# High and low activations as one 512-column operand in the transposed dense products of a two-block kernel

## The chip, the cores and the metric

The kernel runs on one core of a Trainium2 chip. The metric is the device time of one execution in microseconds; less is better. The engines are called as in the profile: PE (TensorE, with PEld for its weight loads), DVE (VectorE), ACT (ScalarE), POOL (GpSimd) and SP (SyncE, which starts the DMAs).

## The reference

The input is x, 256 tokens of 1024 values, and a memory of 256 tokens. Two blocks follow each other, all in fp32. The first has two layers, and the second two hybrid layers (gated sums of three attentions) with projections of their own.

```python
for l in range(DEPTH):
    h = h + 0.5 * swiglu_ffn(rms_norm(h, ffn1_norm[l]), ffn1_w_in[l], ffn1_w_out[l])
    h = h + hybrid_mixer(rms_norm(h, mix_norm[l]), ...)
    h = h + memory_cross_attention(rms_norm(h, xattn_norm[l]), rms_norm(mem, mem_norm[l]), ...)
    h = h + 0.5 * swiglu_ffn(rms_norm(h, ffn2_norm[l]), ffn2_w_in[l], ffn2_w_out[l])
```

`swiglu_ffn` is `(silu(gate) * up) @ w_out` with `gate, up = split(x @ w_in)`, 1024 to 2 x 2816 and back. Most of the arithmetic is such products of 256 tokens with a weight matrix of 1024 or more rows.

## The kernel before

**Precision.** A product x @ w is made of three, with each operand split in a high part, rounded to the matmul's fp32r, and a low part, the rest: high by high, high by low and low by high. Activations are split where they are made (an ACT copy for the high part, a DVE subtraction for the low one). Weights are split as they arrive, by `Weights` (lines 484 to 558): the DMA brings 4 row pieces of 128 at a time into `raw` (three buffers), and `splits` makes of every two pieces a pair `wh` (ACT) and `wl` (DVE), 128x1024 each, in four buffer pairs. A pair comes free when the matmuls that `take` hands it to have been issued.

**Dense steps.** `lin` (605) makes tokens x outputs, with activations as the stationary operand. `lin_T` (631) makes the transposed result, outputs x tokens: weights are the stationary operand, 128x128 a piece, and the 256 tokens of an activation tile (`Xt`, 130) are streamed. For a step of 512 outputs it takes two PSUM banks (`banks_T`, 628), each with two chunks of 128 outputs side by side, and for every row piece c of the weights `chunk_T` (621) makes 4 chunks x 3 matmuls of 256 columns. When all pieces are done, all four chunks are. `lin_halves` (645) is the same over two steps whose row pieces are taken by halves; the output products of mixer, cross attention and hybrid layers use it.

The banks of tag "a" are four (`psa`, 363), so the next step has two of its own while the last one's are emptied. `ps_a` (392) takes one, `give` (389) marks one as free.

**What reads the results.** For each step a `done` function starts a routine that empties the banks two chunks at a time: in `ffn` (819) `gate` multiplies with the broadcast inverse root of the norm (`rsb`, made by `Norm.finish` and `spread`, waited for in `scale_b`) and takes silu; `up` multiplies with that and splits the product for the second matrix; `to_h` (797) scales the output product and adds it to the residual hT, and starts the next norm, whose high and low parts are the next stage's activations. `conv_done`, `sb_done`, `gl_done` and `up_done` do the like in the mixer and in the hybrid layers.

**Order.** A planner (`Plan`, 205) writes the order of all engines while the program is built, from estimated costs (`cost`, 244). Dense matmuls go in program order; the other work, written as routines, is put between them when its inputs are thought to be there. Weight splits have a rank by how far they are ahead: `URG[min(self.next - self.at, len(URG) - 1)]` with `URG = (0, 1, 2)`, lower first, where `next` is the buffer being split and `at` the one that PE takes next (`urgency`, 507). Each engine's queue is then fixed, and an instruction that waits holds up all behind it.

**Stages.** Per layer: 12 feed-forward input steps (gate and up, 512 or 256 outputs, 8 row pieces), 2 output steps (22 row pieces), then the mixer, cross attention and the second feed-forward stage. A hybrid layer makes its projections and attentions, and ends in a tail of six products with 2 or 3 row pieces (`upp`, whose activations u the attentions give) around one step of gates, and an output product.

## Time and profile before

| | |
|---|---|
| median of 3 runs | 1864.98 us (1864.59 to 1865.28) |
| the profiled execution | 1865.29 us |
| its span | 1863.5 us |
| instructions in the span | 35502 |
| matmuls | 14870 |
| mean clock granted to PE | 0.998 of full speed |
| bytes moved | 300.89 MB, a mean of 161 GB/s |

The span is the time from the first to the last instruction that the profile saw. The engines' own lines are among the rows below. Almost all instructions carry line 191, the planner's, so the groups are told apart by the names of their tiles: the tile written stands before the arrow, those read behind it. `pq` is a bank of a transposed step and `pp` one of a step with tokens; a name that ends in h or l is a high or low part, and buffer numbers are left out. A matmul's line gives its start and how long it lasts until its last result; the next one starts before that.

### The profile page before, as it was taken

To read this page: it belongs to the slowest core of one execution; us is meant where nothing else is said; L and a number is where in the kernel's file an instruction comes from. 1 tells how busy PE (TensorE), PEld (TensorE's weight loads), DVE (VectorE), ACT (ScalarE), POOL (GpSimd) and SP (SyncE) were. 2 spreads that over 40 slices of the span, in tenths; PEclk is the share of its full clock that TensorE was granted. 3 is DMA by queue.
4 is the path that set the end of the run, shared out by engine and by line. 5 is a ranking of instruction groups with operands and counts; after the bars stand their busy time and mean duration, and the time that the engine had idled before them with its cause. 6 is when DMAs were issued, how large, how long until landed. Compare 5 with 4: busy or idle time off the path is not lost.

```text
span 1863.5 us, 35502 instructions
## 1 busy us (share of the span) xinstructions
PE 1845.7 (99%) x14870; PEld 1783.5 (96%) x14870; DVE 1257.0 (67%) x2069; ACT 979.7 (53%) x1620; POOL 65.3 (4%) x64
## 2 busy tenths in 40 slices
PE   8999999999999999999999999999999999999999
PEld 8999998889999999999988899999989999999998
DVE  6656786566665565576865666556677868777686
ACT  5445464444544444464645445445576654667553
POOL 0000000000000000000000000000011000101000
PEclk9999999999999999999999999999999999999999
DMA  7546462334554655464633335546545625535633
GB/s 262 186 158 215 141 222 92 113 115 136 166 187 157 194 187 185 149 237 148 204 103 102 113 136 165 185 148 217 153 123 159 231 97 182 163 115 172 206 104 129
DMA packets 169580, 300.89 MB, mean 161 GB/s; under 512 B 7884, under 2 KB 51020, under 8 KB 169292
## 3 DMA queue, kind: packets, MB, share of 16 engines
q1 hardware_dynamic: 169420, 298.63, 49.7%
q8 instruction: 116, 1.90, 0.4%
q14 instruction: 44, 0.36, 0.1%
HBM read 297.56 MB, written 1.05 MB: 160 GB/s over the span
## 4 chain that ended last, share of the span: by engine, by line
PE 96%; DVE 2%; ACT 1%; issue 0%; DMA 0%; POOL 0%; SPq 0%; ACTq 0%; POOLq 0%
PE pq L191 68%; PE pp L191 15%; PE pt L191 2%; PE z L191 1%; PE s L191 1%; PE po L191 1%; PE p L191 1%; PE xs L191 1%; PE xo L191 1%; PE hp L191 1%; PE ep L191 1%; PE mp L191 1%; PE sbo L191 1%; DVE wl L191 0%; PE vp L191 0%; DVE X L191 0%
## 5 line engine op out<-in xcount | busy, mean ns | idle before, releaser
L191 DVE TENSOR_TENSOR wl<-raw,wh 128x1024 fp32r<-128x1024 f32 (+3 forms) x628 | 688.9, 1103 | 369.3 <-ACT wh L191 365.0
L191 ACT ACTIVATE wh<-raw 128x1024 fp32r<-128x1024 f32 (+3 forms) x628 | 598.9, 962 | 534.0 <-PE pq L191 388.6
L191 PE MATMUL pq<-ffn_normh,wh 128*128 128x256 f32 x1408 | 399.2, 284 | 0.1
L191 PE MATMUL pq<-ffn_norml,wh 128*128 128x256 f32 x1408 | 399.1, 283 | 0.0
L191 PE MATMUL pq<-ffn_normh,wl 128*128 128x256 f32 x1408 | 399.0, 283 | 0.0
L191 PEld LDWEIGHTS pq<-ffn_normh,wh 128*128 128x128 f32 x1408 | 270.7, 192 | 0.5 <-ACT ffn_normh L191 0.5
L191 PEld LDWEIGHTS pq<-ffn_norml,wh 128*128 128x128 f32 x1408 | 270.7, 192 | 0.0
L191 PEld LDWEIGHTS pq<-ffn_normh,wl 128*128 128x128 f32 x1408 | 270.6, 192 | 0.0
L191 PE MATMUL pq<-ah,wh 128*128 128x256 f32 x704 | 199.5, 283 | 0.0
L191 PE MATMUL pq<-al,wh 128*128 128x256 f32 x704 | 199.5, 283 | 0.0
L191 PE MATMUL pq<-ah,wl 128*128 128x256 f32 x704 | 199.2, 283 | 0.0
L191 PEld LDWEIGHTS pq<-al,wh 128*128 128x128 f32 x704 | 135.1, 192 | 0.0
L191 PEld LDWEIGHTS pq<-ah,wh 128*128 128x128 f32 x704 | 135.1, 192 | 0.0
L191 PEld LDWEIGHTS pq<-ah,wl 128*128 128x128 f32 x704 | 135.1, 192 | 0.0
L191 PE MATMUL pp<-wh,norm_g_2l 128*128 128x384 f32 (+3 forms) x352 | 118.8, 338 | 0.0
L191 PE MATMUL pp<-wl,norm_g_2h 128*128 128x384 f32 (+3 forms) x352 | 118.4, 336 | 0.3 <-DVE wl L191 0.3
L191 PE MATMUL pp<-wh,norm_g_2h 128*128 128x384 f32 (+3 forms) x352 | 118.1, 335 | 0.0
L191 PE MATMUL pq<-norm_g_2h,wl 128*128 128x256 f32 x384 | 110.6, 288 | 0.4 <-DVE wl L191 0.4
L191 PE MATMUL pq<-norm_g_2h,wh 128*128 128x256 f32 x384 | 110.5, 288 | 0.0
L191 PE MATMUL pq<-norm_g_2l,wh 128*128 128x256 f32 x384 | 109.8, 286 | 0.0
L191 PE MATMUL pq<-mix_normh,wl 128*128 128x256 f32 x320 | 91.6, 286 | 0.0
L191 PE MATMUL pq<-mix_normh,wh 128*128 128x256 f32 x320 | 91.5, 286 | 0.0
(425 smaller groups left out, 3799.1 us busy)
## 6 DMA issues: line engine op xcount, KB each, us to landing
raw<-in_ffn_w_in_dram SPq DMA_DIRECT2D x79, 1024.0 KB, 5.2
raw<-in_w_in_dram SPq DMA_DIRECT2D x48, 1024.0 KB, 5.3
raw<-in_ffn_w_out_dram SPq DMA_DIRECT2D x40, 1024.0 KB, 5.3
raw<-in_w_in_dram SPq DMA_DIRECT2D x28, 768.0 KB, 4.4
raw<-in_xattn_w_kv_dram SPq DMA_DIRECT2D x16, 1024.0 KB, 5.2
raw<-in_w_out_dram SPq DMA_DIRECT2D x16, 1024.0 KB, 5.1
raw<-in_ffn_w_in_dram SPq DMA_DIRECT2D x18, 512.0 KB, 3.5
raw<-in_xattn_w_q_dram SPq DMA_DIRECT2D x8, 1024.0 KB, 5.2
```

The costliest lines, as they stand in the source:

```text
L191: return self.fn(*self.args, **self.kw)
```

## The change

High and low parts of an activation tile become one tile `[128, pieces, 2, 256]`, so that both parts of a row piece are 512 adjacent columns. `lin_T` streams these in one matmul past the high weights, into a whole PSUM bank: columns 0 to 255 gather high by high and, in a second matmul of 256 columns, low weights by high; columns 256 to 511 gather high by low. A step of 512 outputs has four chunks and so takes four banks, one for each. The order of the loops changes: weights are taken in blocks of up to four row pieces (`take4`), and within a block the chunks go one after the other, each with all pieces of the block. A chunk's bank is asked for when its first matmul comes. Both `wh`, `wl` pairs of a block are given back at the block's end. `near` moves `at` on half way through.

Each chunk is reported as full when its last block is done. `joined` then copies its second half out (ACT), adds the first half to it (DVE) and gives the bank back; what used to read PSUM reads that sum. All `done` functions of `lin_T` steps are changed in this way; `gate`, `conv_done`, `sb_done`, `gl_done` and `to_h` wait for `rsb` before it, `up` and `up_done` do not.

Further, keys and values of the memory lie in two tiles each, whose smaller ones are used again for a pair of attention tiles in the hybrid layers; the attention routine `turns` waits for the last unit, no longer the one before it, to have used its transposed weights; and `lin_halves`, which keeps its three matmuls, asks for its second two banks when it comes to them.

```diff
-    def __init__(self, plan, hi, lo):
-        self.plan, self.hi, self.lo, self.ready = plan, hi, lo, {}
...
+    def __init__(self, plan, x):
+        self.plan, self.x, self.hi, self.lo, self.ready = plan, x, x[:, :, 0, :], x[:, :, 1, :], {}
+
+    def both(self, c):
         while c not in self.ready:
             self.plan.idle()
         self.plan.wait(self.ready[c])
-        return self.hi[:, c, :], self.lo[:, c, :]
+        return self.x[:, c]
...
+class Chunks:
+
+
+    def __init__(self, plan, n):
+        self.ps, self.full = [], [plan.flag() for j in range(n)]
...
+        def take4(self, spec):
+
+            w, k0, nk, n0, n = spec
+            for b in blocks([spec]):
+                j0, m = self.at, b[2]
+                js = [j0 + k // 2 for k in range(m)]
...
+                self.at = js[-1]
+
+                def parts(k):
+                    ck.wait(self.ready[js[k]])
+                    return [x[:, k % 2, :n] for x in self.sub_t[js[k]]]
+                yield b[1] - k0, m, parts
+                for j in range(j0, js[-1] + 1):
+                    del self.sub_t[j]
+                    self.free_at["sub", j] = ck.now + 0.2
+                    self.at = j + 1
+                    ck.finish(self.used[j])
+
+        def near(self):
+
+            self.at += 1
...
-        return Xt(ck, xtp.tile([P, 8, S], F32R, tag="xh", name=nm + "h"),
-                  xtp.tile([P, 8, S], F32R, tag="xl", name=nm + "l"))
+        return Xt(ck, xtp.tile([P, 8, 2, S], F32R, tag="x", name=nm))
...
-            ps = banks_T(n)
-            for c, wh, wl in wt.take(spec):
-                xh, xl = x.part(xc + c)
-                chunk_T(ps, n, wh, wl, xh, xl, c == 0, c == nk - 1)
-            done(ps)
+            m = n // P
+            ch = Chunks(ck, m)
+            for k0, nb, parts in wt.take4(spec):
+                if k0 + nb == nk:
+                    done(ch)
+                for j in range(m):
+                    if k0 == 0:
+                        ch.ps.append(ps_a("pq").rearrange("p (a s) -> p a s", a=2))
+                    if j == m // 2:
+                        wt.near()
+                    js = slice(j * P, (j + 1) * P)
+                    for k in range(nb):
+                        wh, wl = parts(k)
+                        c = k0 + k
+                        xb = x.both(xc + c)
+                        dense(mm(ch.ps[j], wh[:, js], xb, c == 0, False, skip=True))
+                        dense(mm(ch.ps[j][:, 0, :], wl[:, js], xb[:, 0, :], False, c == nk - 1, skip=True))
+                    if k0 + nb == nk:
+                        ck.finish(ch.full[j])
...
+    def joined(ch, i, dst):
+
+        for k in range(2):
+            yield ch.full[2 * i + k]
+            ps = ch.ps[2 * i + k]
+            yield A.copy(dst[:, k, :], ps[:, 1, :])
+            yield V.tensor_tensor(dst[:, k, :], ps[:, 0, :], dst[:, k, :], op=OP.add)
+            give("a")
...
-                        yield V.scalar_tensor_tensor(d, ps[i], scale, wide(rb), op0=OP.mult, op1=OP.mult)
-                        give("a")
+                        yield from joined(ps, i, d)
+                        yield V.scalar_tensor_tensor(d, d, scale, wide(rb), op0=OP.mult, op1=OP.mult)
...
-                        yield V.tensor_tensor(sg[i], ps[i], wide(rb), op=OP.mult)
-                        give("a")
+                        yield from joined(ps, i, sg[i])
+                        yield V.tensor_tensor(sg[i], sg[i], wide(rb), op=OP.mult)
...
+                def run(i, xs):
+                    u = k2([P, 2, S], "up")
+                    yield from joined(ps, i, u)
                     yield st["gate"]
...
+                    yield V.tensor_tensor(u, u, st["sg"][i], op=OP.mult)
...
-                    if i > 1:
-                        yield used[i - 2]
+                    if i:
+                        yield used[i - 1]
```

**PE, around the norm's broadcast in the first layer's second feed-forward stage.** `rb` is the broadcast of the norm, the number behind `pq` tells the bank's tile. Before:

```order
L191 MATMUL pq_5482<-ffn2_norml_5263,wh_5396 128x256
L191 MATMUL pq_5482<-ffn2_normh_5262,wl_5397 128x256
L191 MATMUL pq_5482<-ffn2_normh_5262,wh_5396 128x256
L191 MATMUL rb_5481<-cst_94,rs_5467 128x128 x2
L191 MATMUL pq_5482<-ffn2_norml_5263,wh_5396 128x256
L191 MATMUL pq_5482<-ffn2_normh_5262,wl_5397 128x256
L191 MATMUL pq_5483<-ffn2_normh_5262,wh_5396 128x256
L191 MATMUL pq_5483<-ffn2_norml_5263,wh_5396 128x256
L191 MATMUL pq_5483<-ffn2_normh_5262,wl_5397 128x256
```

And now:

```order
L206 MATMUL pq_4789<-ffn2_norm_4671,wl_4729 128x256
L206 MATMUL pq_4789<-ffn2_norm_4671,wh_4747 128x512
L206 MATMUL pq_4789<-ffn2_norm_4671,wl_4748 128x256
L206 MATMUL pq_4789<-ffn2_norm_4671,wh_4747 128x512
L206 MATMUL pq_4789<-ffn2_norm_4671,wl_4748 128x256
L206 MATMUL rb_4850<-cst_94,rs_4844 128x128 x2
L206 MATMUL pq_4875<-ffn2_norm_4671,wh_4803 128x512
L206 MATMUL pq_4875<-ffn2_norm_4671,wl_4804 128x256
L206 MATMUL pq_4875<-ffn2_norm_4671,wh_4803 128x512
```

Three matmuls on a piece, each with a load, are two, four pieces in a row go into one bank, and the broadcast, which stood in the middle of the gate step's successor (16 matmuls in), stands right ahead of that step's first matmul.

**DVE, at the start of the program.** `hT` is the residual, `ffn_norm` the first stage's activations, `acc` the norm's sums of squares, `wl` the weights' low parts. Before:

```order
L191 COPY hT<-pt 128x512 x2
L191 TENSOR_TENSOR wl<-raw,wh 128x1024
L191 SCALAR_TENSOR_TENSOR ffn_norml<-hT,cst,ffn_normh 128x256 x2
L191 COPY hT<-pt 128x512
L191 TENSOR_TENSOR acc<-sq 128x256
L191 SCALAR_TENSOR_TENSOR ffn_norml<-hT,cst,ffn_normh 128x256 x2
L191 TENSOR_TENSOR wl<-raw,wh 128x1024
L191 SCALAR_TENSOR_TENSOR ffn_norml<-hT,cst,ffn_normh 128x256 x2
L191 COPY hT<-pt 128x512
L191 TENSOR_TENSOR wl<-raw,wh 128x1024
L191 SCALAR_TENSOR_TENSOR ffn_norml<-hT,cst,ffn_normh 128x256 x2
```

And now:

```order
L206 COPY hT<-pt 128x512 x2
L206 SCALAR_TENSOR_TENSOR ffn_norm<-hT,cst,ffn_norm 128x256 x4
L206 COPY hT<-pt 128x512 x2
L206 TENSOR_TENSOR acc<-sq 128x256
L206 SCALAR_TENSOR_TENSOR ffn_norm<-hT,cst,ffn_norm 128x256 x4
L206 TENSOR_TENSOR acc<-acc,sq 128x256 x6
L206 TENSOR_TENSOR wl<-raw,wh 128x1024 x3
L206 TENSOR_SCALAR rs<-ssq 128x2
```

The first weights' low parts were third and now stand behind all copies, activations and sums.

**DVE, from the end of the first feed-forward output into the mixer.** `dh` is the scaled output, `mix_norm` the next activations. Before:

```order
L191 SCALAR_TENSOR_TENSOR dh<-pq,rsb 128x512
L191 TENSOR_TENSOR hT<-hT,dh 128x512
L191 SCALAR_TENSOR_TENSOR dh<-pq,rsb 128x512
L191 SCALAR_TENSOR_TENSOR mix_norml<-hT,cst,mix_normh 128x256 x2
L191 TENSOR_TENSOR hT<-hT,dh 128x512
L191 TENSOR_TENSOR acc<-acc,sq 128x256
L191 TENSOR_TENSOR wl<-raw,wh 128x1024
L191 SCALAR_TENSOR_TENSOR mix_norml<-hT,cst,mix_normh 128x256 x2
L191 TENSOR_TENSOR acc<-acc,sq 128x256
L191 TENSOR_TENSOR wl<-raw,wh 128x1024
```

And now:

```order
L206 TENSOR_TENSOR dh<-pq,dh 128x256 x2
L206 SCALAR_TENSOR_TENSOR dh<-dh,rsb 128x512
L206 TENSOR_TENSOR hT<-hT,dh 128x512
L206 TENSOR_TENSOR dh<-pq,dh 128x256 x2
L206 SCALAR_TENSOR_TENSOR mix_norm<-hT,cst,mix_norm 128x256 x2
L206 SCALAR_TENSOR_TENSOR dh<-dh,rsb 128x512
L206 TENSOR_TENSOR acc<-acc,sq 128x256
L206 TENSOR_TENSOR wl<-raw,wh 128x1024
L206 TENSOR_TENSOR hT<-hT,dh 128x512
L206 TENSOR_TENSOR acc<-acc,sq 128x256
L206 TENSOR_TENSOR wl<-raw,wh 128x1024
L206 SCALAR_TENSOR_TENSOR mix_norm<-hT,cst,mix_norm 128x256 x2
```

Four adds have come in. Where one weight split stood ahead of the last low parts, behind the last sum into hT, there are two now, one ahead of that sum and one behind it.

## Rows read from the trace of the kernel before

**Rows 1.** The page, part 1: busy us, share of the span and instructions of each engine.

```profile
PE 1845.7 (99%) x14870; PEld 1783.5 (96%) x14870; DVE 1257.0 (67%) x2069; ACT 979.7 (53%) x1620; POOL 65.3 (4%) x64
```

**Rows 2.** The page, part 4: the chain that ended last, share of the span by engine.

```profile
PE 96%; DVE 2%; ACT 1%; issue 0%; DMA 0%; POOL 0%; SPq 0%; ACTq 0%; POOLq 0%
```

**Rows 3.** Waits of PE: us in total, times, longest us.

```profile
PE pt L191 <- DMA h<-in_x_dram: 6.5, 3, 4.2
PE hp L191 <- DVE fs L191: 2.6, 2, 1.6
```

**Rows 4.** Timeline of PE near 100 us: start us, us, engine, line, op, tiles, shape.

```profile
100.06 0.28 PE L191 MATMUL pq<-ffn_norml,wh 128*128 128x256 f32 x1
100.18 0.28 PE L191 MATMUL pq<-ffn_normh,wl 128*128 128x256 f32 x1
...
101.98 0.28 PE L191 MATMUL pq<-ffn_normh,wl 128*128 128x256 f32 x1
```

**Rows 5.** Timeline of PE near 350 us, a token step of 512 columns.

```profile
350.04 0.39 PE L191 MATMUL pp<-wh,memxl 128*128 128x512 f32 x1
350.27 0.39 PE L191 MATMUL pp<-wh,memxh 128*128 128x512 f32 x1
...
351.40 0.39 PE L191 MATMUL pp<-wh,memxl 128*128 128x512 f32 x1
```

**Rows 6.** Instructions that read tile wl: xcount, duration ns min/median/max, starts, forms.

```profile
L191 PE MATMUL pq<-ffn_normh,wl x1408: 278/283/415, 11.3 to 1261.8; 128*128 128x256 f32 x176
L191 PE MATMUL pq<-ah,wl x704: 278/283/288, 139.4 to 1325.2; 128*128 128x256 f32 x176
L191 PE MATMUL pq<-norm_g_2h,wl x384: 277/283/387, 1452.5 to 1820.9; 128*128 128x256 f32 x192
...
L191 PE MATMUL pq<-mix_normh,wl x320: 278/283/366, 204.5 to 937.0; 128*128 128x256 f32 x160
L191 PE MATMUL pq<-memxh,wl x128: 278/283/364, 299.7 to 1004.9; 128*128 128x256 f32 x128
```

**Rows 7.** DVE groups by form: xcount, busy us, mean ns, idle before them.

```profile
L191 DVE TENSOR_TENSOR wl<-raw,wh 128x1024 fp32r<-128x1024 f32 x452 | 550.4, 1222 | 319.2 <-ACT wh L191 317.3 <-PE pq L191 0.6
...
L191 DVE TENSOR_TENSOR acc<-acc,sq 128x256 f32<-128x256 f32 x66 | 27.0, 420 | 0.6
```

**Rows 8.** ACT groups by form, the same columns.

```profile
L191 ACT ACTIVATE wh<-raw 128x1024 fp32r<-128x1024 f32 x452 | 474.8, 1056 | 448.9 <-PE pq L191 339.7 <-PE pp L191 30.9 <-issue 26.3
...
L191 ACT COPY rsb<-rb 128x256 f32<-128x256 f32 x9 | 3.2, 373 | 5.7 <-PE rb L191 5.7
```

**Rows 9.** Stretches of mixer, feed-forward input and tail: us, busy us (instructions), clock, DMA.

```profile
core 0: us, PE busy (x) PEld busy (x) DVE busy (x) ACT busy (x) POOL busy (x), PEclk, DMA share, GB/s
204.00:297.00 93.00, 93.00 (x841) 89.14 (x840) 77.98 (x141) 47.52 (x83) 5.23 (x3) 1.00 0.49 155
669.00:796.00 127.00, 127.00 (x1061) 127.00 (x1061) 77.68 (x90) 60.91 (x75) 0.70 (x1) 1.00 0.53 171
...
1529.00:1569.00 40.00, 39.91 (x333) 39.28 (x332) 35.30 (x68) 21.11 (x35) 0.00 (x0) 1.00 0.44 145
```

**Rows 10.** Timeline of DVE at the start of the program.

```profile
9.03 1.23 DVE L191 TENSOR_TENSOR wl<-raw,wh 128x1024 fp32r<-128x1024 f32 x1 [0.95 <-ACT wh L191]
...
22.51 0.87 DVE L191 TENSOR_TENSOR acc<-acc,sq 128x256 f32<-128x256 f32 x2
```

**Rows 11.** Timeline of DVE at the end of the first feed-forward output.

```profile
203.76 0.69 DVE L191 SCALAR_TENSOR_TENSOR dh<-pq,rsb 128x512 f32<-128x512 f32 x1
...
208.72 0.87 DVE L191 SCALAR_TENSOR_TENSOR mix_norml<-hT,cst,mix_normh 128x256 fp32r<-128x256 f32 x2
```

**Rows 12.** Timeline of PE: first matmuls of the mixer and of the second feed-forward stage.

```profile
204.28 0.28 PE L191 MATMUL pq<-mix_normh,wh 128*128 128x256 f32 x1
...
477.52 0.28 PE L191 MATMUL pq<-ffn_normh,wh 128*128 128x256 f32 x1
```

**Rows 13.** Timeline of ACT in the second feed-forward stage: the norm's broadcast.

```profile
492.04 0.37 ACT L191 COPY rsb<-rb 128x256 f32<-128x256 f32 x1 [1.37 <-PE rb L191]
```

More of the change, by code (lines that the diff above doesn't have):

```diff
@@ L139, in part, with append, both @@
         self.plan.wait(self.ready[c])
-        return self.hi[:, c, :], self.lo[:, c, :]
+        return self.x[:, c]
+    def part(self, c):
+        x = self.both(c)
+        return x[:, 0, :], x[:, 1, :]
 class Blocks:
     def __init__(self):
-        self.blocks = []
-    def part(self, c):
-        return self.blocks[c // 4].part(c % 4)
+        self.at = []
+    def append(self, x, n):
+        self.at += [(x, c) for c in range(n)]
+    def both(self, c):
+        x, i = self.at[c]
+        return x.both(i)
+class Chunks:
+    def __init__(self, plan, n):
+        self.ps, self.full = [], [plan.flag() for j in range(n)]
 class Proc:
@@ L542, in splits @@
                 ck.finish(self.ready[j])
+        def take4(self, spec):
[3 more added lines that the diff above has]
+                js = [j0 + k // 2 for k in range(m)]
+                assert all(self.raws[self.subs[j][0]][1:] == b[1:] for j in js)
+                self.at = js[-1]
[10 more added lines that the diff above has]
+            self.at += 1
         def take(self, spec):
@@ L650, in body @@
             x = get_x()
-            ps = [[ps_a("pp") for t in range(2)] if tokens else banks_T(512) for n in range(2)]
+            ps = []
             for kh in range(2):
                 for n in range(2):
+                    if not kh:
+                        ps.append([ps_a("pp") for t in range(2)] if tokens else banks_T(512))
                     for c, wh, wl in wt.take(specs[2 * kh + n]):
@@ L874, in run @@
                     for i in range(2):
-                        yield V.tensor_tensor(cin[:, 2 * i:2 * i + 2, :], ps[i], wide(rb), op=OP.mult)
-                        give("a")
+                        ci = cin[:, 2 * i:2 * i + 2, :]
+                        yield from joined(ps, i, ci)
+                        yield V.tensor_tensor(ci, ci, wide(rb), op=OP.mult)
                     co = k4([P, 4, S], "conv")
@@ L1312, in run @@
                     for i in range(2):
-                        yield A.copy(mem["k"][:, 4 * n + 2 * i:4 * n + 2 * i + 2, :], ps[i])
-                        give("a")
+                        h = 2 * n + i
+                        yield from joined(ps, i, mem["k"][h // 3][:, 2 * (h % 3):2 * (h % 3) + 2, :])
                 mem["kp", n] = ck.spawn(run())
@@ L1326, in run @@
                 for t in range(2):
-                    yield A.copy(mem["v"][:, t, n * 512:(n + 1) * 512], ps[t])
+                    for h in range(2 * n, 2 * n + 2):
+                        yield A.copy(mem["v"][h // 3][:, t, h % 3, :], ps[t][:, 256 * (h % 2):256 * (h % 2) + 256])
                     give("a")
@@ L1351, in run @@
                     for i in range(2):
-                        yield A.copy(qT[:, 2 * i:2 * i + 2, :], ps[i])
-                        give("a")
+                        yield from joined(ps, i, qT[:, 2 * i:2 * i + 2, :])
                     ck.finish(st["qf"][g])
@@ L1951, in run @@
                     for i in range(2):
-                        yield V.tensor_tensor(g[:, 2 * i:2 * i + 2, :], ps[i], wide(rb), op=OP.mult)
-                        give("a")
+                        gi = g[:, 2 * i:2 * i + 2, :]
+                        yield from joined(ps, i, gi)
+                        yield V.tensor_tensor(gi, gi, wide(rb), op=OP.mult)
                     for j in range(4):
@@ L1977, in run @@
                 def run(k):
+                    y = k2([P, 2, S], "y")
+                    yield from joined(ps, k, y)
                     yield st["g_p", n, b]
```

55 lines of the change are left out of this document (28 added, 27 removed).

## The prediction

> **What bounds the kernel now.** I read the page's busy times first: TensorE (PE) is busy 99% of the 1863.5 us span, VectorE (DVE) 67%, ScalarE (ACT) 53% [rows 1]. A busy PE need not be a PE at its peak, so next comes the chain that ended last: 96% of it is PE work [rows 2]. Then the waits of PE alone: the largest entry is the first load of the program, 6.5 us, and the next is 2.6 us [rows 3]. So the time is what PE's own instructions take, and only what shortens their stream, or makes PE wait, moves it.
>
> The stream itself is seen in a stretch of the first feed-forward stage: matmuls of 256 columns start 0.120 us apart (100.06 to 101.98 is 16 steps) [rows 4], though each lasts 0.28 us, since they are pipelined. Matmuls of 512 columns, in another stage, start 0.2267 us apart (350.04 to 351.40 is 6 steps) [rows 5]. Twice the columns cost 0.1067 us more, so a matmul here costs 0.1067 us for 256 columns and some 0.0133 us that does not depend on them.
>
> **What the change removes.** A transposed dense step makes three matmuls of 256 columns for each piece of 128 x 128 weights: high weights with high activations, high weights with low, low weights with high. Now the first two are one matmul of 512 columns. The three took 3 x 0.120 = 0.360 us; the two take 0.2267 + 0.120 = 0.3467. The matmuls with low weights count the pieces: 1408 + 704 + 384 + 320 and three groups of 128 (of which one stands) [rows 6], so 3200; the mixer's, the cross-attention's and the last layers' output products keep three matmuls. 3200 x 0.0133 = **42.7 us less on PE**, all of it on the path.
>
> A page of the Trainium skill speaks against this: TensorE: Matmul & The Clock Gate, section "Back-to-back issue gap", gives a warm gap of columns / 2.4 + 2.5 ns. By that rule a merge saves 2.5 ns, 3200 of them 8 us, and the sum below would end at 1886. The trace disagrees: the rule gives 109 and 216 ns where the trace has 120 and 227 [rows 4, 5].
>
> **What it adds off the path.** High and low halves land side by side in one bank, so each 128-output chunk now needs a ScalarE copy and a VectorE add before its old first operation, which then reads SBUF. That is 376 of each. The nearest rows: a copy of 128x256 out of PSUM takes 0.373 us [rows 8], an add of 128x256 0.420 [rows 7]; so 140 us on ACT and 158 on DVE. In a feed-forward input stage, DVE goes from 77.7 us of 127 [rows 9] to 77.7 + 44 x 0.42 = 96 of 122, and stays hidden. Two things decide it there. A bank is wanted again three chunks after it filled: 3 x 4 x 0.3467 = 4.2 us, against copy and add with one weight split ahead on each engine, 0.37 + 0.42 + 1.06 + 1.22 = 3.1 [rows 7, 8]. And both weight buffers of a block of four k pieces come free only at its end, so two new splits have 5.5 us, against about 1.06 + 3 x 1.22 = 4.7 with some copies and adds between. Both fit, with 1 us to spare; I charge nothing. If either failed, PE would wait in every block.
>
> **Where PE will wait.** Six kinds of place, by the order of the changed program.
>
> *The start.* VectorE's first weight split stood third and began at 9.03 us [rows 10]; now it stands behind all four copies of hT, the eight low halves and all seven sums. The reason is in the code: the step sets `at` to its second buffer before the first is split, `next - at` is -1, and Python takes the last, lowest rank. Before, the last of those sums ended at 22.51 + 0.87 = 23.4 with six splits of 1.22 ahead of it [rows 7, 10]; without them, and without the 0.95 of idle in the first of these rows, that is 15.1, so the first split begins, and PE's stream with it, 6.1 us later than before. **+6**, bounds 4 and 8: ScalarE's queue, reordered alike, may hold DVE up for less than that 0.95 or for 2 us more.
>
> *Four ends of a feed-forward output* into the next stage. Chunks 6 and 7 of the normed activations come last. Before, their low halves ended at 208.72 + 0.87 = 209.6 [rows 11], 5.3 us after the next stage began at 204.28 [rows 12]; they were wanted after 6 x 12 x 0.12 = 8.6. Now pieces are taken four at a time, so chunk 6 is wanted after 18 pairs, 18 x 0.3467 = 6.2 us; the chain has a copy and two adds more and, in the new order, a weight split more: 5.3 + 0.37 + 0.84 + 1.22 = 7.7. **4 x 1.5 = +6**, bounds 0 and 12 (the planner's order leaves other slots, or a second split stands in the way).
>
> *The gate after cross attention* (two places). Four chunks now hold all four banks, and the gate's code waits for the norm's broadcast `rsb` before its first copy. Before, rsb ended at 492.04 + 0.37 = 492.4 [rows 13], 14.9 us after the stage began [rows 12]; the first step lasted 96 x 0.12 = 11.5, but the second had two other banks. Now the second step starts at 11.1 and needs one. The new order puts the broadcast's matmuls behind the 64th dense one, the step's last, so that nothing covers what follows: rsb 0.37, copy 0.37, add 0.42 [rows 7, 8], 1.2 in all, and I allow 0.8 for the broadcast's own matmuls and the hand-overs. **2 x 2 = +4**, bounds 0 and 6. At three other such gates they stand 5 dense matmuls earlier: **3 x 0.5 = +1.5**, bounds 0 and 4.5.
>
> *Between the halves of a feed-forward output* the same extra split delays a weight block: **4 x 0.5 = +2**, bounds 0 and 4.
>
> *The tail of the last two layers and the mixers.* In the tail DVE was busy 35.3 of 40 us; 28 chunks add 11.8, so 47 against 40 - 96 x 0.0133 = 38.7 us of PE [rows 9], 8 too much. The last sums, some 5 us, are wanted only in the second half of the output product, so I take **2 x 2.5 = +5**, bounds 0 and 14. In the mixer, 78.0 of 93 [rows 9] and 20 chunks more are 86 of 91, near the limit but under it: **2 x 2 = +4**, bounds 0 and 10. The attention's second buffer of transposed weights is given up too; its chain is hidden by the dense work around it, and what it costs if that cover is short lies in the tail's bound.
>
> Edits with one answer: splitting the keys and values of the memory into two tiles moves copies of the same size; the output products take their second pair of banks later, which can only spare a wait of which rows 3 show none. Loads are the same ones in the same order.
>
> **Sum.** Added: 6 + 6 + 4 + 1.5 + 2 + 5 + 4 = 28.5. The profiled execution took 1865.3 us (1863.5 of span), 0.3 over the median of the runs: 1865.3 - 42.7 + 28.5 = 1851.1, said as **1851**. With every low bound (only the start lost) it is 1865.3 - 42.7 + 4 = 1827; with every high one, 1865.3 - 42.7 + 58.5 = 1881.
>
> **Rivals.** (a) *The planner hides nearly all.* It places work by estimated times and had PE waiting for almost nothing before [rows 3]; then only the start is lost: 1865.3 - 42.7 + 6 = 1829. Against it: the four slips at stage ends come from the order itself. Chance 0.15.
> (b) *The waits eat the gain.* Tail and mixer are at DVE's limit; at their high bounds the sum gains 24 - 9 = 15 us: 1866. Chance 0.11.
> (c) *Slower: weight splits come late in every block.* Four pairs of split buffers, two held for a whole block, leave 1 us; if the copies and adds of a block's evictions push the second split past the point where PE wants it, by 0.3 us in half of the 200 blocks, that is 30 us more: 1881. It decides as soon as the work between release and second split passes 6.2 us. For it: every split's DVE part follows its ACT part on a queue that has grown. Against: 96 of 122 us in the feed-forward stages. Chance 0.11.
> (d) *The merge saves nothing*, if 0.120 us is the rate at which such columns stream and 512 of them take 0.240: 1865.3 + 28.5 = 1894. Against it: 0.2267 [rows 5]. Chance 0.03. The page's rule named above would end near it, at 1886.
> (e) *My forecast*, 1836 to 1861: 0.60.
>
> **How the numbers follow.** About 0.2% is what a measurement can tell from no change, 3.7 us. Faster: (e) and (a), 0.75. Same: (b), 0.11. Slower: (c) and (d), 0.14. For eight in ten I leave out the lower half of (a) and all of (c) and (d): 1829 to 1867.
>
> **What would show it.** Starts of 0.227 and 0.120 us by turns in a feed-forward stage; 3200 matmuls fewer; PE idle for about 5 us more before 17 us, released by DVE's wl; short PE waits some 6 us into a stage, on a norm's low halves, and at 11 us on a bank; DVE over 90% in the tail. Waits on wl all through the feed-forward stages would mean (c); starts of 0.240, (d).

## The result, and the profile after

The changed kernel takes 1898.2 us (median of 4 runs, 1896.4 to 1901.6) against 1865.1 before: ratio 1.0179, 95% interval 1.0161 to 1.0196. It is slower by 33 us where 14 us less was forecast, and lies above the range. The profiled execution took 1899.5 us, 34 more than the one before.

First the page of the kernel after, busy times and the shares of the chain that ended last:

```profile
PE 1842.0 (97%) x11670; PEld 1616.2 (85%) x11670; DVE 1383.3 (73%) x2449; ACT 1073.6 (57%) x1992; POOL 66.3 (3%) x64
...
PE 87%; DVE 7%; ACT 3%; issue 2%; DMA 1%; POOL 0%; SPq 0%; ACTq 0%; DVEq 0%; POOLq 0%
```

PE's share of the chain fell from 96% [rows 2] to 87%; DVE and ACT held 3% and now hold 10%. In the span PE stands for 1897.7 - 1842.0 = 55.7 us, where it stood for 17.8 before; and it is busy only 3.7 us less, though a merge was to save it over 40. The waits of PE (total, times, longest; answers to [rows 3]):

```profile
PE pq L206 <- DVE wl L206: 10.1, 16, 1.9
PE pq L206 <- ACT wh L206: 7.1, 6, 3.9
PE pq L206 <- DVE sg L206: 5.7, 3, 2.6
...
PE pq L206 <- DVE mix_norm L206: 3.1, 2, 1.5
```

Three kinds are new or have grown from a few tenths: weight splits (wl, wh), banks that the gate's eviction holds (sg), and activations at a stage's start (mix_norm). By the first matmul of each stage in the two traces, in us:

| Stage | pieces in the new form | before | after |
|---|---|---|---|
| up to the first dense matmul | | 9.4 | 14.3 |
| four FFNs | 2112 | 769.4 | 767.4 |
| two mixers with memory | 448 | 421.5 | 427.4 |
| two cross attentions | 128 | 124.9 | 124.5 |
| two hybrid layers, to the last product | 512 | 534.3 | 560.3 |

So 26 of the 34 us between the two profiled executions are lost in the two hybrid layers. In them it is the stretch of the gate products, from the last token step to the first up product, beside which the attentions run: 78.5 us in each layer before, 89.5 and 92.3 after, 24.9 more. (By the same starts the projections ahead of it give back 3.4 us in the two layers, the up products and the output product behind it cost 1.9 and 2.6.) The stretches before, then after (columns as in [rows 9]):

```profile
1451.40:1529.80 78.40, 78.20 (x642) 75.39 (x640) 56.66 (x112) 45.34 (x92) 1.49 (x1) 1.00 0.52 173
1718.00:1796.40 78.40, 78.20 (x642) 75.38 (x641) 56.66 (x112) 45.33 (x92) 1.49 (x1) 1.00 0.51 172
```

```profile
1459.90:1549.40 89.50, 83.23 (x494) 69.74 (x492) 66.62 (x136) 52.96 (x115) 1.47 (x1) 0.96 0.45 147
1736.40:1828.70 92.30, 84.81 (x494) 71.14 (x491) 66.22 (x137) 52.48 (x114) 1.46 (x1) 0.94 0.44 145
```

PE has 148 instructions fewer there and is yet busy 5 to 7 us longer, beside 6 to 7.5 us in which it stands. A large part of that is the granted clock, 0.96 and 0.94 where it was 1.00: 0.04 of 89.5 us and 0.06 of 92.3 are 3.6 and 5.5 us, by estimate.

How a stop begins is seen at the first gate block. PE:

```profile
1463.02 0.48 PE L206 MATMUL pq<-norm_g,wh 128*128 128x512 f32 x1
1465.44 0.39 PE L206 MATMUL pq<-norm_g,wl 128*128 128x256 f32 x1 [1.95 <-DVE wl L206]
```

and DVE beside it:

```profile
1461.19 1.21 DVE L206 TENSOR_TENSOR wl<-raw,wh 128x1024 fp32r<-128x1024 f32 x1
...
1463.47 0.48 DVE L206 SCALAR_TENSOR_TENSOR nq<-pt,cst,nq 64x256 fp32r<-64x256 f32 x1 [0.60 <-ACT nq L206]
...
1464.17 1.22 DVE L206 TENSOR_TENSOR wl<-raw,wh 128x1024 fp32r<-128x1024 f32 x1
```

The first chunk of a block reads all four weight pieces, so both buffer pairs, within its first 1.4 us. The block's second split is ready at 1465.4, some 2 us after PE wants it; ahead of it in DVE's queue stood work of the attentions (nq). Piece by piece the second pair was first wanted after 24 matmuls, 2.9 us on. No earlier block of four holds a buffer here, so at this place it is the early demand alone. The late return shows in ACT's waits, first before, then after, in the first layer's stretch:

```profile
ACT wh L191 <- PE pq L191: 11.2, 7, 2.2
```

```profile
ACT wh L206 <- PE pq L206: 10.0, 4, 4.6
ACT gt L206 <- PE pq L206: 9.8, 11, 1.9
```

ACT's weight copies (wh) waited for PE's buffers before as well, and as long in total; but now one stands up to 4.6 us, until PE has finished a block, where it was 2.2. The eleven waits of bank copies (gt) for PE's chunks, in the same queue, are new. PE waits for the splits, ACT for PE.

And what a stop can cost beyond itself, at the gate behind the cross attention:

```profile
498.50 0.76 PE L206 MATMUL pq<-ffn_norm,wh 128*128 128x512 f32 x1 [2.62 <-DVE sg L206]
...
499.27 0.63 PE L206 MATMUL pq<-ffn_norm,wh 128*128 128x512 f32 x1
...
499.91 0.63 PE L206 MATMUL pq<-ffn_norm,wh 128*128 128x512 f32 x1
```

```profile
498.50:501.20 2.70, 2.70 (x9) 2.32 (x10) 1.68 (x5) 1.34 (x4) 0.00 (x0) 0.50 0.66 192
501.20:504.00 2.80, 2.80 (x17) 2.44 (x17) 0.65 (x1) 0.63 (x1) 0.00 (x0) 0.98 0.49 189
```

After 2.6 us of standing, the granted clock is 0.50 (the level of 1.2 GHz) for 2.7 us: a pair takes 0.64 us and not 0.35, which costs some 1.2 us more. Not every such stop does this. In e12, an experiment below, the same stop of 2.62 us ends at 497.98 and the clock stays at 1.00, with 15 matmuls in the next 2.7 us and not 9:

```profile
497.98:500.68 2.70, 2.70 (x15) 2.39 (x16) 1.67 (x5) 1.35 (x4) 0.00 (x0) 1.00 0.74 228
```

Over the whole span the mean granted clock was 0.993, and 0.998 before: 13.3 and 3.7 us lost to it, by estimate, so nearly 10 of the 34 us. What decides whether a stop is followed by the low level is not shown.

### The profile page after: what moved, and what is told of

The parts are those of the page before. It is cut to its first block, busy times and chain, and to the rows that moved or that the text cites. A ratio compares the mean times of both kernels' runs of the same rounds, so it can differ in the third digit from the quotient of the medians.

```text
span 1897.7 us, 29714 instructions
## 1 busy us (share of the span) xinstructions
PE 1842.0 (97%) x11670; PEld 1616.2 (85%) x11670; DVE 1383.3 (73%) x2449; ACT 1073.6 (57%) x1992; POOL 66.3 (3%) x64
## 4 chain that ended last, share of the span: by engine, by line
PE 87%; DVE 7%; ACT 3%; issue 2%; DMA 1%; POOL 0%; SPq 0%; ACTq 0%; DVEq 0%; POOLq 0%
PE pq L206 62%; PE pp L206 12%; DVE wl L206 3%; PE pt L206 2%; ACT wh L206 1%; PE z L206 1%; PE s L206 1%; PE po L206 1%; PE p L206 1%; PE xo L206 1%; PE xs L206 1%; DMA raw<-in_w_in_dram 1%; PE ep L206 1%; PE mp L206 1%; PE sbo L206 1%
## 5 line engine op out<-in xcount | busy, mean ns | idle before, releaser
L206 PE MATMUL pq<-ffn_norm,wh 128*128 128x512 f32 x1408 | 500.9, 401 | 11.5 <-DVE sg L206 5.7
L206 PE MATMUL pq<-ffn_norm,wl 128*128 128x256 f32 x1408 | 396.3, 281 | 0.1
L206 PEld LDWEIGHTS pq<-ffn_norm,wh 128*128 128x128 f32 x1408 | 266.6, 189 | 78.3 <-issue 5.6
L206 PEld LDWEIGHTS pq<-ffn_norm,wl 128*128 128x128 f32 x1408 | 267.6, 190 | 0.1
L206 PE MATMUL pq<-act,wh 128*128 128x512 f32 x704 | 247.9, 397 | 1.1 <-DVE dh L206 1.1
L206 PE MATMUL pq<-act,wl 128*128 128x256 f32 x704 | 197.4, 280 | 0.0
L206 PE MATMUL pp<-wh,norm_g 128*128 128x384 f32 (+3 forms) x704 | 183.1, 335 | 3.7 <-ACT norm_g L206 1.5
L206 PEld LDWEIGHTS pq<-act,wh 128*128 128x128 f32 x704 | 132.1, 188 | 33.4 <-DVE dh L206 2.4
L206 PE MATMUL pq<-norm_g,wh 128*128 128x512 f32 x384 | 146.4, 416 | 3.2 <-ACT wh L206 3.2
L206 PEld LDWEIGHTS pq<-act,wl 128*128 128x128 f32 x704 | 132.8, 189 | 0.0
```

Of the source, the lines that this page charges most:

```text
L206: return self.fn(*self.args, **self.kw)
```

## What a pair of matmuls takes

The forecast's saving was read from starts of 0.2267 us [rows 5]. In the changed kernel near 100 us, in the stage of [rows 4]:

```profile
99.89 0.40 PE L206 MATMUL pq<-ffn_norm,wh 128*128 128x512 f32 x1
100.13 0.28 PE L206 MATMUL pq<-ffn_norm,wl 128*128 128x256 f32 x1
...
101.30 0.40 PE L206 MATMUL pq<-ffn_norm,wh 128*128 128x512 f32 x1
```

From 99.89 to 101.30 are four pairs: 0.353 us each, not 0.3467. Elsewhere in the same trace pairs do take 0.347. Over all runs of three pairs in one of the two rhythms, 762 of 2625 go at 347 ns and 1863 at 353, so the mean saving is 0.29 x 13.3 + 0.71 x 6.7 = 8.6 ns, and 3200 pieces save 27.5 us, if those in between go alike. The change therefore lost 34 + 27.5 = 62 us on its way, where 28.5 were charged.

## Experiments

The theories at first: **hold** (a block of four pieces keeps both buffer pairs to its end, and the next split waits in ACT's queue), **rank** (late splits get the planner's lowest rank), **load** (too many copies and adds). Results together; the last column is the sum of the two gate stretches, 156.9 us before:

| Run | median, us | ratio to before, 95% interval | gate stretches, us |
|---|---|---|---|
| the change | 1898.2 | 1.0179, 1.0161 to 1.0196 | 181.8 |
| e1 | 1910.9 | 1.0234, 1.0215 to 1.0252 | 179.6 |
| e2 | 1932.9 | 1.0354, 1.0338 to 1.0370 | 188.8 |
| e3 | 1928.6 | 1.0342, 1.0324 to 1.0360 | 163.2 |
| e4 | 1885.6 | 1.0098, 1.0081 to 1.0115 | 164.5 |
| e5 | 1892.6 | 1.0140, 1.0122 to 1.0158 | 167.7 |
| e6 | 1907.2 | 1.0213, 1.0188 to 1.0237 | 172.6 |
| e7 | 1897.1 | 1.0166, 1.0151 to 1.0181 | 185.7 |
| e8 | 1904.0 | 1.0197, 1.0174 to 1.0220 | 179.8 |
| e9 | 1931.9 | 1.0346, 1.0325 to 1.0368 | 172.3 |
| e10 | 1877.7 | 1.0058, 1.0042 to 1.0074 | 160.7 |
| e11 | 1876.6 | 1.0050, 1.0032 to 1.0069 | 159.8 |
| e12 | 1870.8 | 1.0023, 1.0010 to 1.0037 | 158.3 |
| e13 | 1889.9 | 1.0119, 1.0104 to 1.0135 | 184.6 |
| e14 | 1859.6 | 0.9961, 0.9949 to 0.9974 | 159.8 |
| e15 | 1859.4 | 0.9962, 0.9948 to 0.9976 | 161.0 |
| e16 | 1898.6 | 1.0169, 1.0152 to 1.0186 | 184.7 |

**e1, the rank mended.**

```diff
-            return URG[min(self.next - self.at, len(URG) - 1)]
+            return URG[max(0, min(self.next - self.at, len(URG) - 1))]
```

> Edit: the urgency of the weight splits is cut off at rank 0 (when the index next minus at is negative, the list is no longer read from its end), nothing else. The trace of the changed kernel loses about 25 us in the two gate stretches of the hybrid layers (78.5 us before, 89.5 and 92.3 us after) and about 5 us at the start, where the first dense matmul starts at 14.32 us and not at 9.44 us. Theory rank (splits that are late get the lowest rank and so stay late): both go, 1868 us. Theory hold (a block of four weight pieces keeps both of its buffer pairs until its end, and the next split stands at the head of ACT's queue with copies behind it): only the start comes back, 1893 us. Theory load (the added copies and adds themselves are too much for ACT and DVE there): 1893 us as well.

The first dense matmul came at 11.0 us instead of 14.3, but the stage behind it ended at 145.4, 2.2 us later than in the change: the splits now delayed the norm's scale. The gate stretches hardly moved, so theory rank falls for them. That the whole is 13 us slower comes from the up products behind them: they take 49.2 and 48.6 us in the two layers, and some 39.5 and 42.7 in the change, with the same work in another order. In the first layer PE waits there for the attention's outputs (u) and for banks (y):

```profile
PE pq L206 <- DVE y L206: 3.4, 4, 1.7
PE pq L206 <- DVE u L206: 3.2, 2, 2.1
```

**e2, the merge undone.**

```diff
-                        dense(mm(ch.ps[j], wh[:, js], xb, c == 0, False, skip=True))
+                        for s in range(2):
+                            dense(mm(ch.ps[j][:, s, :], wh[:, js], xb[:, s, :], c == 0 and s == 0, False, skip=True))
```

> Edit: the chunk order, the banks and the added copies and adds stay, but the 512-column matmul is again two of 256 columns into the two halves of the bank. In the changed trace a clean pair of matmuls takes 353 ns, in the trace before three 256-column matmuls took 360 ns. If that is all, 3200 pieces times 0.0067 us is +21 us: 1919 us. If the prediction's 0.0133 us a piece is right after all: +43 us, 1941 us. If the slower matmuls only use up time in which PE now waits for weights, less than +21 us: down to 1898 us.

+35 us by the medians, 29 by the spans of the two profiled executions: between the two figures, as the mixture of rhythms would have it (27.5). With 256 columns alone, undisturbed starts are 0.120 us apart, in this kernel as before. So the merge itself is worth about 28 us, and what comes with it (chunk order, banks, copies and adds) costs about twice that.

**e3, two pieces at a time.**

```diff
-            for b in blocks([spec]):
-                j0, m = self.at, b[2]
-                js = [j0 + k // 2 for k in range(m)]
+            for q in range(0, nk, 2):
+                j0, m = self.at, min(2, nk - q)
+                js = [j0] * m
```

> Edit: the chunk order runs over two weight pieces at a time and not four, so each buffer pair goes back after half a block (2.8 us and not 5.6 us); all four chunk banks of a step stay open until its end. Theory hold: the gate stretches come back to about 80 us and the first split is no longer behind, 1870 us. Theory rank: the index is no longer negative either, so the same, and the kernel with the rank mended alone tells the two apart. Theory load: the same number of copies and adds, so nothing in the gate stretches, and later banks at the step ends: 1898 us or up to 10 us more.

The gate stretches fall from 181.8 to 163.2 us, as hold says. The whole is 30 us slower, 20 more than any theory allowed, and the FFNs pay: all four banks of a step are full only in its last 2.8 us, and PE waits 44 times for one:

```profile
PE pq L206 <- DVE sg L206: 26.7, 44, 2.1
```

**e4, the old form for the gate products alone** (`lin_old` is `lin_T` of the kernel before).

```diff
-            lin_T(nx, w, 3986 + b * D + n * 512, 512, gl_done(n, b))
+            lin_old(nx, w, 3986 + b * D + n * 512, 512, gl_done(n, b))
...
-                        yield from joined(ps, i, gi)
-                        yield V.tensor_tensor(gi, gi, wide(rb), op=OP.mult)
+                        yield V.tensor_tensor(g[:, 2 * i:2 * i + 2, :], ps[i], wide(rb), op=OP.mult)
+                        give("a")
```

> Edit: only the six gate products of each hybrid layer (12 of the 116 products) go back to the form before, piece by piece, 256 columns, two banks, no copy and add. If the loss of the gate stretches comes from the form of these products (theories hold, rank and load alike), they return to about 79 us each: -25 us, less 384 pieces times 0.0067 us = 2.6 us: 1876 us. If it comes from the attention beside them, whose second transposed buffer the change gave up (each turn waits for the one ahead), the stretches stay at about 90 us: 1898 us.

-12.6 us of the 22 expected: half of the loss of the hybrid layers is made by these 12 products (by the starts in the two traces, 14.4 of 26). The waits on weights are gone from the stretch; in their place PE waits for the attention's outputs (u), which the wait on weights had hidden:

```profile
PE s L206 <- DVE u L206: 2.3, 1, 2.3
PE pq L206 <- DVE u L206: 2.1, 1, 2.1
PE pq L206 <- DVE wl L206: 0.2, 1, 0.2
```

**e5, two pieces at a time in the gate products alone** (the edit of e3, for these products).

```diff
+            for q in range(0, nk, 2 if pairs else 4):
+                j0, m = self.at, min(2 if pairs else 4, nk - q)
...
+            lin_T(nx, w, 3986 + b * D + n * 512, 512, gl_done(n, b), pairs=True)
```

> Edit: only the six gate products of each hybrid layer run over two weight pieces at a time and so give a buffer pair back after 2.8 us and not 5.6 us; matmuls, copies and adds are those of the changed kernel, and the FFN keeps its blocks of four. Theory hold: the gate stretches (89.5 and 92.3 us) come down to the 81 us that the same order showed in the kernel with two pieces everywhere, with their banks a little later: 1898 - 20 = 1878 us, at least 1885. Theory load: 1898 us.

The stretches fall by 14 us with the same matmuls, copies and adds, so the block of four pieces is shown to be the cause there. A block of two both asks for one pair less at once and gives its pair back sooner, and this run doesn't tell the two apart. ACT's waits went with it (compare above):

```profile
ACT wh L206 <- PE pq L206: 10.3, 9, 2.2
ACT gt L206 <- PE pq L206: 1.4, 5, 0.3
```

The median fell by 5.6 only, below the 13 to 20 expected. Half of what the stretches gained is lost behind them: in the first layer the up products run at a mean granted clock of 0.93 and take 44.2 us, not 39.6.

**e6, the attention's second buffer back.**

```diff
-                    if i:
-                        yield used[i - 1]
+                    if i > 1:
+                        yield used[i - 2]
```

> Edit: the attention of the hybrid layers has its second transposed buffer back (a turn waits for the use before the last one, as in the kernel before), all else as changed. If the serial turns are part of the loss, the waits of the attention's products on the transposed copies (0.7 us twice) and the stalls behind them go: -2 to -8 us, 1890 to 1896 us. If they are hidden, 1898 us. If the buffer is missed by something else (the pool is shared with the copies), up to 1903 us.

The stretches fall by 9 us, and it is given back at once: in the first layer PE stands 4.5 us before 1589.7 for the output product's activations, and no time is gained. The median is 9 us up; the trace is of the fastest of the four executions, 1899.1 us, so where the others lost that isn't shown. Alone the buffer moves the wait.

**e7, copy and add ahead of the norm's scale** (here the gate; the convolution and the mixer products alike).

```diff
-                    rb = yield from nx.scale_b()
...
+                    rb = None
...
                         yield from joined(ps, i, sg[i])
+                        rb = rb or (yield from nx.scale_b())
```

> Edit: in the gate, convolution and mixer products the bank is copied and added before the norm's scale is waited for, so that the bank is given back without it; only the multiplication waits. Theory bank (the two waits of 2.6 us at 498.5 and 1156.9 us, behind the scale after the cross attention, are of banks held): both go, and the smaller ones at 681 us and 216 us do not, as those wait for the norm's split: -5 us, 1893 us. If PE then stops for something else that is late there (the gate's activation before the first up product), 1898 us.

The two waits shrank from 2.6 to 2.0 us and no further; nothing to be measured in the time. So the scale holds the bank for 0.6 us of the 2.6, and something else for the rest.

**e8, four matmuls of 512, then four of 256.**

```diff
                         dense(mm(ch.ps[j], wh[:, js], xb, c == 0, False, skip=True))
+                    for k in range(nb):
+                        wh, wl = parts(k)
```

> Edit: inside a chunk of four weight pieces first the four 512-column matmuls, then the four 256-column ones, where the changed kernel takes them by turns. In the changed trace a pair by turns takes 353 ns, against 227 + 120 = 347 ns by the starts of each kind among its own in the trace before. Theory turn (each change of width costs about 3 ns): a chunk has 2 changes in place of 8, so 4 x 0.347 + small = 1.39 against 1.41 us: 800 chunks x 0.02 = -16 us, 1882 us. Theory sum (the 512-column matmul takes 0.233 in this place anyway): 1898 us. The low halves of the weights are also needed up to 0.7 us later, which may take some of the waits on them away.

No gain. In the timeline of this kernel a chunk of eight starts 1.40 us after the one before it (704.75 to 706.15), which is 0.350 a piece, with mean starts of 0.233 (704.75 to 705.68) and 0.118. Over all undisturbed chunks the mean is 0.351, as in the changed kernel, where pairs by turns go at 0.347 in some stages: it is not the change of width that costs. This trace loses 12 us in the hybrid layers, whose up products take 49.4 and 50.6 us.

```profile
704.75 1.09 PE L206 MATMUL pq<-ffn_norm,wh 128*128 128x512 f32 x4
705.68 0.63 PE L206 MATMUL pq<-ffn_norm,wl 128*128 128x256 f32 x4
706.15 1.09 PE L206 MATMUL pq<-ffn_norm,wh 128*128 128x512 f32 x4
```

**e9, one DVE reduction for copy and add.**

```diff
-            yield A.copy(dst[:, k, :], ps[:, 1, :])
-            yield V.tensor_tensor(dst[:, k, :], ps[:, 0, :], dst[:, k, :], op=OP.add)
+            yield V.tensor_reduce(dst[:, k, :], ps.rearrange("p c d -> p d c"), axis=AX.X, op=OP.add)
```

> Edit: the two halves of a chunk's bank are joined by one DVE reduction straight out of PSUM (the form of ut from po, 0.68 us for the same 256 outputs out of 512) in place of an ACT copy (0.37 us) and a DVE add (0.42 us): 376 copies leave ACT, DVE gains 376 x 0.26 = 98 us of busy time. Theory hold with ACT's queue in the middle (a weight copy that waits for its buffer stands ahead of the bank copies): no bank copy is left in that queue, so the gate stretches fall from 90 us towards 80 us, and every stage end has one step less: 1875 us. Theory load (too much eviction work, DVE the fuller engine): DVE is fuller still and the gate stretches grow: 1905 to 1915 us.

Both theories get their part: the gate stretches, without bank copies in ACT's queue, fall by 9.5 us, but the time rises by 34, of which 12 ahead of the hybrid layers. A join now takes 0.68 us of DVE:

```profile
L206 DVE TENSOR_REDUCE up<-pq 128x256 f32<-128x512 f32 x88 | 58.9, 684 | 4.0 <-PE pq L206 3.5
```

and the up products, where DVE was nearest its limit, go from 39.6 to 54.3 us in the first layer. That load decides there is argued, not shown: in e1 and e8 the same products rose to 49 us and more by order alone.

**e10, e4 and e6 together.**

> Edit: the kernel with the old gate products, and the second transposed buffer of the attention back as well. Its gate stretches were 82 us each (78.5 us before), with waits of 2.3 us of the scores on the attention's gathering and 2.1 us of the next products on it. If the serial turns set those once the weights do not: -3 to -5 us a layer, 1877 us against 1885.6 us. If not, 1886 us.

-8 us against e4. In the hybrid layers it is 4.5: with weights in time the serial turns did set the end; the 2.3 us are gone and the 2.1 are 0.9. The other half lies ahead of these layers, which began at 1331.0 and not 1335.9, in code that is the same in both; this execution had 1388 runs of three pairs at 347 ns, and that of e4 had 690.

**e11, the hybrid layers as before; e12, all but the FFNs as before.** The edit of e4 for the up products too, then for convolution, mixer, memory and query products, with the buffer of e6:

```diff
-            lin_T(lambda: st["u"], a[nm][l], n * 512, 512, up_done(n, i, b), nk, c0)
+            lin_old(lambda: st["u"], a[nm][l], n * 512, 512, up_done(n, i, b), nk, c0)
```

> Edit: both hybrid layers as in the kernel before (gate and up products piece by piece, second transposed buffer), all else as changed. The two layers took 535 us before and 560 us changed. If all of that loss is made by what the change does inside them: -26 us, 1872 us. If part of it comes from the new tiles around them (memory tiles that now lend their place to the key transposes, joined activation tiles), less: 1875 to 1880 us.

> Edit: only the four FFNs keep the new form (2112 of the 3200 pieces); mixers, memory, cross attention and hybrid layers go piece by piece again. By the stage table of the changed kernel the FFNs took 767.4 us against 770.8 us before, though 2112 x 0.0067 = 14 us was there to be saved, and the first dense matmul started 4.9 us later. Theory ends (the saving is eaten by the start, by 1.5 us at each FFN end and 2.6 us at the gate behind the cross attention): before + 5 - 3 = 1867 us, within 3 us. If what is lost in the FFNs comes from the new form of their neighbours, 1857 us.

In e11 the two layers take 538 us by the same starts, against 534 before and 560 in the change. e12 is 6 us below e11 and still not below the kernel before. Its FFNs take 6.2 us less than before, its start is 5.5 us later, and the stages in the old form lose 3.3: most of what is left is lost inside the FFNs and at the start, as theory ends has it.

**e13, the first gate and up step of each FFN in the old form; e14, the same on e12; e15, e14 with the planner's matmul time 11.3 ns longer.**

```diff
-            lin_T(nx, w_in, n0, n, gate)
-            lin_T(nx, w_in, DFF + n0, n, up)
+            (lin_T if n0 else lin_old)(nx, w_in, n0, n, gate)
+            (lin_T if n0 else lin_old)(nx, w_in, DFF + n0, n, up)
```

> Edit: on the changed kernel, only the first gate step and the first up step of each FFN (8 of the 116 products) go back to the form before: piece by piece, two banks, no copy and add. Theory stage start (a chunk of the new order asks for four activation pieces, with their low halves, and four weight pieces within its first 1.4 us, and its bank for a copy and an add behind the norm's scale): the start comes back from 14.3 to about 9.5 us, the two waits of 2.6 us and one of 1.5 us go, 256 pieces lose about 8 ns each: -5 - 5.2 - 1.5 + 2 = -10 us, 1888 us. If those waits only move to the second step: 1900 us.

> Edit: as the kernel in which only the FFNs are changed (1870.8 us), with the first gate and up step of each FFN in the form before as well. Theory stage start: -10 us again: 1860 us, faster than before by 5 us. If the waits move to the second step: 1871 us.

> Edit: the kernel with only the FFNs changed but for their first steps, and the planner's time for a matmul longer by 11.3 ns (its 256 columns then cost 120 ns as in the trace, its 512 columns 227 ns, where it reckoned 109 and 215 ns). If the planner's clock that runs ahead makes it issue copies and splits too early into ACT's and DVE's queues, fewer waits and -2 to -5 us against the kernel without: 1856 us. If not, the same 1860 us, or worse where the order shifts, 1865 us.

e13 gains 8.3 us on the change (14 up to the hybrid layers, of which these lose 5 again). The first dense matmul starts at 8.52 us, and the waits on sg leave the list of PE's waits:

```profile
8.52 0.58 PE L206 MATMUL pq<-ffn_norm,wh 128*128 128x256 f32 x1
```

e14 gains 11 us on e12 and is **faster than both kernels**, by 0.39% (0.26 to 0.51) against before. Its FFNs, with 1856 pieces in the new form, take 10.7 us less than before, and the start and the stages in the old form lose half of it. The planner's times (e15) make no difference.

**e16, the changed kernel again, unedited.**

> Edit: none, the changed kernel once more. If the rhythm of 347 or 353 ns belongs to the program: 347 ns again in the two stretches from 502 to 671 us and from 1160 to 1332 us and 353 ns elsewhere, and single times within 0.1% of each other. If it belongs to the execution: other stages at 347 ns, and single times from about 1894 us (most at 347) to 1903 us (most at 353), as 2600 pieces times 6.7 ns is 17 us between the two ends.

Near 100 us, in the stage that went at 353 ns:

```profile
99.71 0.40 PE L206 MATMUL pq<-ffn_norm,wh 128*128 128x512 f32 x1
...
101.10 0.40 PE L206 MATMUL pq<-ffn_norm,wh 128*128 128x512 f32 x1
```

1.39 us for four pairs, 0.347 each. In this execution 1600 of 2614 go at 347 ns. The rhythm belongs to the execution, and a stage that has begun in one keeps it until PE stops, be it for 0.05 us (at 692.0 in the trace of the change), or until matmuls of another kind come between. The single times, 1894.4 to 1901.3, scatter as expected; yet this one, the one with the profile, was the slowest, since it lost 6 us more in the hybrid layers at a granted clock of 0.93 to 0.96. So the rhythm alone doesn't order the times.

## Why the prediction was wrong

The step from the page to "PE's own stream is the time" was right for the kernel before, and e2 bears out that the merge shortens that stream. Two steps failed: the price of the merge, taken as 13.3 ns a piece, and the charge of nothing for the gate products and the attention beside them. The forecast missed by 47 us (1898 against 1851), and of that:

- **The saving per piece**, 13.3 ns for each of 3200: it is 13.3 or 6.7, mean 8.6 in the profiled execution. That term is 27.5 and not 42.7 us, 15 of the miss. The price came from one stretch at 0.2267 [rows 5]. The same kernel before has 512-column starts of 0.230 to 0.236 in about a third of its undisturbed places; their mean of some 0.229 would still have given 11 ns, so the mixture of widths has a price of its own. Rival (d), that the merge saves nothing, gave 1894 us, 4 from the time measured; that was luck, since e2 shows the merge to save 28. By the rule cited from the Trainium skill (TensorE: Matmul & The Clock Gate, "Back-to-back issue gap"), which the page gives for an isolated matmul, a merge saves 2.5 ns. No run agrees with it: even the slow rhythm saves 6.7.
- **The tail and the attention's buffer**, 5 us: the two hybrid layers lost 26 us, 30 with the saving added. The prediction looked for the loss in the tail, by DVE's share there. That share came (38.2 of 39.6 us in the up products), and up and output products together lost 4.5, close to the 5. It charged the gate products nothing, and of the attention beside them it said "its chain is hidden by the dense work around it". There 24.9 us were lost, and e4, e5 and e10 show by what: weight pairs wanted two at once and held to a block's end (with the gate products in the old form the stretches fall from 181.8 to 164.5, with blocks of two to 167.7), then the serial turns (to 160.7, of 156.9 before). Some 25 of the miss. Rival (c) had this mechanism, with the margin of 1 us for splits, but in every block; the FFN's blocks kept their margin, while in the gate stretches the attentions take DVE and ACT between two splits. How the 14 us of e5 divide between early demand and late return isn't shown, and of them only 5.6 reach the time.
- **The clock** stood in no term: by the mean granted clocks it took nearly 10 us more than before, an estimate, which is part of the losses in the other terms. Some stops are followed by a stretch at half pace, 1.2 us dearer in the one shown, and others are not.
- *The start*, 6: it is 4.9 (14.32 against 9.44). The size was right and so was the reason: DVE's first split began at 15.72, where 15.1 was forecast, and with the rank mended the first dense matmul came at 11.0 (e1). But the 3.3 us were lost again in the same stage; with the order by pieces in the first steps the start is as early as before, and stays so (e13).
- *Four ends*, 1.5 each: PE stands 1.5 us at 215.8, 681.0, 873.8 and 1343.0, as forecast (with 1.1 more at 1339.4). *The gate behind cross attention*, 2 each: 2.6 standing and 1.2 of slow clock, so 3.8. The prediction put it down to the broadcast of the scale, which is 0.6 of it (e7); the rest goes when the first two steps have the old form (e13), which takes away the four banks, the early demand and the copies and adds together. *Between the halves*, 0.5 each: PE waits 0.2 to 0.3 us at each, and for a bank (dh), not for weights.
- *Mixers*, 4: by the table they take 5.9 us longer. With 448 x 8.6 ns = 3.9 of saving that is 9.8 lost, of which 3 are two of the four ends, so some 7. (e12 against e11 gives 5.8, with cross attention taken in.)
- *Nothing charged in FFN blocks*: right. From 30 to 140 us PE has no idle time at all, with copies of 0.37 and adds of 0.42 us as reckoned from [rows 7, 8]:

```profile
30.00:140.00 110.00, 110.00 (x624) 95.36 (x624) 80.44 (x112) 63.49 (x102) 0.00 (x0) 1.00 0.53 172
```

The FFNs as a whole still keep only 2.0 us of a saving of 18 (2112 x 8.6 ns). Of the 16 lost, some 10 are the waits and the slow clock listed here; where the rest goes is open.

Of its signs, the matmuls by turns, the 3200 matmuls fewer, the idle time at the start (most of it ended by ACT's wh, not by DVE's wl) and the waits on a norm's low halves came, DVE over 90% in the tail too, and the bank wait 12.5 us into the stage (at 495.9, in one that began at 483.4).

## What to carry to other kernels

An order that reads all weight pieces of a block for one output chunk wants its inputs sooner and gives its buffers back later than an order by pieces; in the stretch of FFN blocks shown it cost nothing, at a stage's start and beside the attentions it cost more than the merge gave. Keep the old order for the first steps and for stretches shared with other work, and use the new one where an engine's stream is all there is (e14). Take a matmul's price in the mixture of widths that will run, as a mean over many stretches, and allow in the range for a slow clock behind a stop.

## What the runs showed that was not expected

Dense pairs run in steps: three 256-column matmuls take 360.0 ns, a 512 with a 256 takes 353.3 or 346.7, which are 864, 848 and 832 cycles of 2.4 GHz, 16 apart. Which of the two a stage gets differs between executions of the same program (e16) and holds until PE stops or other matmuls come between; an all-256 stream (e2, before) has one rhythm. What chooses it stays open, and so does what makes the clock fall behind one stop of 2.62 us and not behind another.
